# The norm of a Conformer module in another order, with its tap diagonals made inside the module

## Chip, cores, metric

One core of a Trainium2 chip. The metric is the device time of one execution in microseconds (us).

## What is computed

Two trunk layers over 256 latent tokens of 1024 channels. Layer 0 mixes tokens with a state-space scan, layer 1 with a Conformer convolution module; each is followed by a gated feed-forward network (FFN 0, FFN 1), and a norm ends it. The change lies in layer 1's module and touches the end of FFN 0:

```python
def conformer_conv_module(h, rows, w_pw1, b_pw1, dw_w, dw_b, ln_g, ln_b, w_pw2, b_pw2):
    u = h @ w_pw1 + b_pw1
    u = u[..., :CONF_DIM] * jax.nn.sigmoid(u[..., CONF_DIM:])
    v = dwconv1d(u, dw_w, dw_b) if rows is None else axial_dwconv(u, rows, dw_w, dw_b)
    v = jax.nn.silu(layernorm(v, ln_g, ln_b))
    return v @ w_pw2 + b_pw2
```

The 256 tokens form 4 grid rows of 64. `axial_dwconv` runs 31 taps along the grid row for channels 0 to 511 (horizontal) and along the 4 rows for channels 512 to 1023 (vertical). `layernorm` goes over the 1024 channels of a token.

## The kernel before

**Products.** Every large product is done as three matmuls on split operands (`mm3`): high part by high part (L293), low part of one by high part of the other (L294) and the reverse (L295). A weight tile of 128x1024 goes through four steps: SP loads it into one of four raw buffers, `wraw` (L267); ACT casts it to the high part `wh` (L269); DVE subtracts to get the low part `wl` (L282); TensorE uses both. A raw buffer is free again when its `wl` has been written, so each load waits for the subtraction four weights back. SP, ACT and DVE each work in the order of their queue.

**The module (`conformer`).** The 1024 channels are 8 blocks of 128; blocks 0 to 3 are horizontal, 4 to 7 vertical. The first projection (`w_pw1`) yields two blocks with their gates at a time; `gated` turns them around with TensorE transposes of `ug`, ACT takes the sigmoid `sig` (L1124) and DVE multiplies (L1126) into `upad` (blocks 0 to 3, with a margin) or `uver` (blocks 4 to 7). Vertical taps are done on DVE (L1107) after a first one on ACT (L1104). Of the horizontal taps, block 0's and part of block 3's are done on DVE (L1157, in the even sum `cv` and the odd sum `odd`, added on L1159; first ones on ACT, L1153 and L1155). Those of blocks 1 and 2, and the rest of block 3's, are done on TensorE (`horizontal`, L1177): `upad` is written to DRAM (L1166), read back in four shifted copies `u4` (L1168), and 32-column matmuls with diagonal matrices as weights sum the taps in PSUM. ACT (L1181, blocks 1 and 2) or DVE (L1183, block 3) moves the sum to `cv`. A call of `horizontal` takes a range of grid rows: two rows are 128 tokens, one half of the tokens.

**The diagonals.** `taps` makes three tiles of 128x1024, one each for blocks 1, 2 and 3, from the tap weights `dwx` (three DVE operations, L1086). It runs in FFN 0's second projection and puts them into buffers of the pool `ar`, which otherwise takes the weights of the modulation vectors that are worked out in the background (`araw`, loads on L368). The pool is held from FFN 0 to the end.

**The norm.** A `LayerNorm` for each half of the tokens. The table of strings `LNO` sets the order on TensorE, DVE, ACT and GpSimd, by tokens of a letter, the half (for `h` the block), and the part:

- `s`: TensorE transposes two blocks of `cv`, DVE takes their statistics (L195)
- `r`: mean and variance (L199, L451) and the root on GpSimd (L444)
- `m`: DVE normalizes 256 channels (L205)
- `c`: TensorE turns these back, ACT applies gain, bias and SiLU to give `modv` (L217)
- `x`: DVE splits `modv` into high and low part, `xmh` and `xml` (L298, L299)
- `h`: a call of `horizontal`; `t`: ACT loads its SiLU table (L1219)
- `W`, `w`: load and cast, and subtraction, of one weight of the second projection (`w_pw2`)

Ahead of it `CO` lists one call, block 1, grid rows 0 and 1; the rest of the taps are `h` tokens. Outside such a written order a scheduler places instructions by priority. `LF` lists which weights, by number, are held behind a mark (`behind`, used on the cast and on the subtraction); the hold acts on the queue of the engine that the mark is on, DVE. The second projection (`project`, with bias rows from L554) takes its first four weights half by half: all of the first half of the tokens, then the second.

## Time and profile before

| | |
|---|---|
| time, median of 3 | 886.54 us (884.85 to 888.57) |
| time of the profiled execution | 884.54 us |
| its span | 882.7 us |
| mean granted TensorE clock | 0.991 |
| busy: TensorE, DVE, ACT, GpSimd | 851.3, 663.5, 501.2, 48.6 us |
| module, end of first projection to end of second | 630 to 682 us |

The profile is of one execution. Times in its views count from the start of the span; the device time is a little longer than the span. A row of the chain of waits has start, length, and what it was. A row of a timeline has start, length, engine, line, operation, output and inputs with the shape, the number of instructions in it, and in brackets how long the engine stood ahead of it and what released it. A matmul's length includes its way through the array, so starts, not lengths, tell the rate. PE is TensorE.

### The profile page before, as it was taken

To read this page: it belongs to the slowest core of one execution; us is meant where nothing else is said; L and a number is where in the kernel's file an instruction comes from. 1 tells how busy PE (TensorE), PEld (TensorE's weight loads), DVE (VectorE), ACT (ScalarE), POOL (GpSimd) and SP (SyncE) were. 2 spreads that over 40 slices of the span, in tenths; PEclk is the share of its full clock that TensorE was granted. 3 is DMA by queue.
4 is the path that set the end of the run, shared out by engine and by line. 5 is a ranking of instruction groups with operands and counts; after the bars stand their busy time and mean duration, and the time that the engine had idled before them with its cause. 6 is when DMAs were issued, how large, how long until landed. Compare 5 with 4: busy or idle time off the path is not lost.

```text
span 882.7 us, 12690 instructions
## 1 busy us (share of the span) xinstructions
PE 851.3 (96%) x4632; PEld 649.3 (74%) x4634; DVE 663.5 (75%) x1096; ACT 501.2 (57%) x847; POOL 48.6 (6%) x77
## 2 busy tenths in 40 slices
PE   8999999999999999989999999999989999999996
PEld 4576776767777777767888777878767788888885
DVE  3378689797878989789998898777966895555434
ACT  4286988597687887374444434566354754444421
POOL 1001011101001010110000000010001000000000
PEclk9999999999999999999999999999989999999999
DMA  9757856658455455458999989828545497555521
GB/s 347 310 169 252 261 187 215 215 168 262 151 185 167 144 181 178 164 185 312 376 346 337 331 321 324 285 72 281 159 148 187 150 337 252 180 179 189 189 74 48
DMA packets 55872, 194.59 MB, mean 220 GB/s; under 512 B 6665, under 2 KB 9169, under 8 KB 54786
## 3 DMA queue, kind: packets, MB, share of 16 engines
q1 hardware_dynamic: 54338, 190.00, 63.0%
q0 software_dynamic: 896, 2.28, 0.8%
q10 hardware_dynamic: 576, 1.51, 0.5%
q8 instruction: 36, 0.59, 0.3%
q14 instruction: 26, 0.21, 0.1%
HBM read 191.94 MB, written 1.82 MB: 220 GB/s over the span
## 4 chain that ended last, share of the span: by engine, by line
PE 71%; DVE 14%; ACT 6%; DMA 5%; issue 2%; POOL 1%; SPq 0%; POOLq 0%; DVEq 0%; ACTq 0%
PE acc L295 19%; PE acc L294 19%; PE acc L293 19%; DVE wl L282 3%; DVE bx L739 3%; PE ps L251 3%; PE pa L342 2%; ACT wh L269 2%; PE ps L987 2%; PE ps L1017 1%; PE ps L1177 1%; DMA wraw<-in_w_pw_dram 1%; DMA wraw<-in_w_z_dram 1%; PE ps L1025 1%; DMA emat<-edram 1%
## 5 line engine op out<-in xcount | busy, mean ns | idle before, releaser
L282 DVE TENSOR_TENSOR wl<-wraw,wh 128x1024 fp32r<-128x1024 f32 (+2 forms) x226 | 267.4, 1189 | 94.8 <-ACT wh L269 93.8
L269 ACT CAST wh<-wraw 128x1024 fp32r<-128x1024 f32 (+2 forms) x226 | 227.7, 1016 | 154.7 <-PE acc L295 60.0
L293 PE MATMUL acc<-wh,xmh 128*128 128x512 f32 x544 | 219.0, 403 | 1.6 <-ACT bx L732 1.6
L295 PE MATMUL acc<-wh,xml 128*128 128x512 f32 x544 | 214.6, 395 | 0.9 <-DVE xml L299 0.8
L294 PE MATMUL acc<-wl,xmh 128*128 128x512 f32 x544 | 214.7, 395 | 0.5 <-DVE wl L282 0.4
L293 PEld LDWEIGHTS acc<-wh,xmh 128*128 128x128 f32 x544 | 102.5, 188 | 29.0 <-issue 4.4
L295 PEld LDWEIGHTS acc<-wh,xml 128*128 128x128 f32 x544 | 102.4, 188 | 26.5 <-DVE xml L299 3.2
L294 PEld LDWEIGHTS acc<-wl,xmh 128*128 128x128 f32 x544 | 102.7, 189 | 23.0 <-DVE wl L282 1.8
L293 PE MATMUL acc<-xmh,wh 128*128 128x512 f32 (+1 forms) x192 | 77.6, 404 | 0.1
L295 PE MATMUL acc<-xmh,wl 128*128 128x512 f32 (+1 forms) x192 | 75.4, 396 | 1.2 <-DVE wl L282 1.2
L294 PE MATMUL acc<-xml,wh 128*128 128x512 f32 (+1 forms) x192 | 75.6, 394 | 0.0
L739 DVE SCALAR_TENSOR_TENSOR bx<-bxraw,pc,bx 128x508 f32<-128x508 f32 (+1 forms) x96 | 69.8, 766 | 5.4 <-ACT bx L732 5.2
L294 PE MATMUL acc<-wl,midh 128*128 128x512 f32 x176 | 69.6, 395 | 0.6 <-DVE wl L282 0.6
L295 PE MATMUL acc<-wh,midl 128*128 128x512 f32 x176 | 69.1, 393 | 0.0
L382 DVE SCALAR_TENSOR_TENSOR araw<-araw,srow 128x1024 f32<-128x1024 f32 x56 | 67.9, 1216 | 0.0
L293 PE MATMUL acc<-wh,midh 128*128 128x512 f32 x176 | 65.9, 394 | 0.0
L293 PEld LDWEIGHTS acc<-xmh,wh 128*128 128x128 f32 (+1 forms) x192 | 35.7, 186 | 13.6 <-issue 5.1
L295 PEld LDWEIGHTS acc<-xmh,wl 128*128 128x128 f32 (+1 forms) x192 | 35.5, 186 | 10.8 <-DVE wl L282 1.9
L294 PEld LDWEIGHTS acc<-xml,wh 128*128 128x128 f32 (+1 forms) x192 | 35.8, 186 | 8.3 <-issue 1.0
L294 PEld LDWEIGHTS acc<-wl,midh 128*128 128x128 f32 x176 | 33.0, 188 | 9.8 <-DVE wl L282 2.5
L293 PEld LDWEIGHTS acc<-wh,midh 128*128 128x128 f32 x176 | 33.0, 188 | 7.4
L295 PEld LDWEIGHTS acc<-wh,midl 128*128 128x128 f32 x176 | 33.0, 188 | 7.3
(236 smaller groups left out, 1084.1 us busy)
## 6 DMA issues: line engine op xcount, KB each, us to landing
wraw<-in_ffn_in_dram SPq DMA_DIRECT2D x88, 512.0 KB, 5.0
araw<-in_ada_wt_dram SPq DMA_DIRECT2D x56, 512.0 KB, 5.2
wraw<-in_ffn_out_dram SPq DMA_DIRECT2D x44, 512.0 KB, 3.9
wraw<-in_w_xb_dram SPq DMA_DIRECT2D x32, 384.0 KB, 4.0
wraw<-in_ada_w_dram SPq DMA_DIRECT2D x24, 512.0 KB, 4.4
emat<-edram SPq DMA_DIRECT2D x8, 1536.0 KB, 7.9
wraw<-in_w_pw_dram SPq DMA_DIRECT2D x24, 512.0 KB, 4.8
araw<-in_ada_dram SPq DMA_DIRECT2D x16, 512.0 KB, 8.4
```

Source lines behind the costliest of these rows:

```text
L251: self.nc.tensor.transpose(out, in_, self.ident[0:n, 0:n])
L269: nc.scalar.copy(out=wh[:, :n], in_=raw[:, :n])
L282: self.nc.vector.tensor_tensor(out=wl, in0=raw, in1=wh.bitcast(F32), op=ALU.subtract)
L293: mm(out=out, lhsT=ah, rhs=bh, start=first, stop=False)
L294: mm(out=out, lhsT=ah, rhs=bl, start=False, stop=False)
L295: mm(out=out, lhsT=al, rhs=bh, start=False, stop=last)
L342: self.nc.tensor.matmul(out=pa[32 * j:32 * j + 32, 0:n], lhsT=self.sc[:, k, :], rhs=rhs(j), start=k == 0, stop=k == KD - 1, tile_position= ...
L382: self.nc.vector.scalar_tensor_tensor(out=raw, in0=raw, scalar=1.0, in1=self.srow, op0=ALU.mult, op1=ALU.mult, accum_out=col[:, k])
L739: nc.vector.scalar_tensor_tensor(out=o[:, :, a:b], in0=r[:, :, a + d:b + d], scalar=w(k), in1=o[:, :, a:b], op0=ALU.mult, op1=ALU.add)
L987: nc.tensor.matmul(out=ph, lhsT=bt[:, tt], rhs=xw[:, tt], start=tt == 0, stop=tt == 1)
L1017: nc.tensor.matmul(out=po[64 * j:64 * j + 64, d * 256:d * 256 + 256], lhsT=h0[:, d, c], rhs=cc, start=True, stop=True, tile_position=(0, 6 ...
L1025: nc.tensor.matmul(out=py[64 * j:64 * j + 64, p2, q * P:q * P + P], lhsT=xs[:, tt, hl * 64:hl * 64 + 64], rhs=e[:, hl, slot], start=slot i ...
```

## The change

It has five parts. First, the diagonals are made in the module, in a tile of its own (`dk`): two after the second `upad`, one after the fourth; `taps` goes, and `dwx` is loaded in the module. Second, the pool `ar` is opened anew in each FFN. Third, block 1 is done in one call with all four grid rows (256 columns), and `h11` goes. Fourth, the tokens `W` and `w` go from `LNO`: the weights of the second projection come from `project` alone, the first held behind the mark `m01`, the second behind `x00`, the other six behind `x01` (before, the last four behind `x01`, and the first four where their tokens stood). Fifth, the rest of `LNO` is put in another order: block 3's second part and the statistics of the second half come before `x01`.

```diff
-LF = (4, 8, "x01"),
+LF = (0, 1, "m01"), (1, 2, "x00"), (2, 8, "x01")
...
-CO = (1, 0, 2),
-LNO = "W0 w0 W1 w1 s02 s12 h20 h30 t00 s03 s00 s01 r00 W2 W3 s13 h11 m00 c00 m01 w2 c01 h21 x00 w3 s10 x01 m02 c02 m03 c03 x02 x03 h31 s11 r10 m10 c10 m11 c11 x10 m12 x11 m13 c12 x12 c13 x13"
+CO = (1, 0, 4),
+LNO = "s02 s12 h20 h30 t00 s03 s00 s01 r00 s13 h21 m00 c00 m01 c01 h31 x00 s10 s11 r10 x01 m02 c02 m03 c03 x02 x03 m10 c10 m11 c11 x10 m12 x11 m13 c12 x12 c13 x13"
...
-    def ffn(self, es, l, xh, xl, h, mid, then, quiet=None):
+    def ffn(self, es, l, xh, xl, h, mid, then):
         nc, t = self.nc, self.t
+        self.ar = es.enter_context(self.tc.tile_pool(name="ar", bufs=AR))
...
-            if k == kn - QUIET and quiet:
-                self.settle()
-                quiet()
-            wh, wl = ready[k] if k < len(ready) else self.weights(wsrc[k], (1, 1024), spare.get(k))
+            wh, wl = self.weights(wsrc[k], (1, 1024), spare.get(k))
...
-    def taps(self):
-
-
-        nc = self.nc
-        dwx = self.sb.tile([P, P], F32, name="dwx")
-        nc.sync.dma_start(out=dwx, in_=self.t["dwx"])
-        self.dk = []
-        for b in (1, 2, 3):
-            self.dk.append(self.ar.tile([P, 1024], F32, name="araw").rearrange("p (i c) -> p i c", i=32))
-            nc.vector.tensor_tensor(out=self.dk[-1], in0=self.diag.unsqueeze(1).broadcast_to([P, 32, 32]),
-                                    in1=dwx[:, b * 32:b * 32 + 32].unsqueeze(2).broadcast_to([P, 32, 32]), op=ALU.mult)
-
...
+        dk = cp.tile([P, 3, 32, 32], F32, name="dk")
...
+        dwx = cp.tile([P, P], F32, name="dwx")
+        nc.sync.dma_start(out=dwx, in_=t["dwx"])
...
+                i = nc.vector.scalar_tensor_tensor(out=u[:, :, 15:79] if blk < 4 else u, in0=rows(pt[:, 0:256]),
+                                                   scalar=col(PC_BPW1 + blk), in1=rows(sig), op0=ALU.add, op1=ALU.mult)
...
+            for b in ((1, 2), (3,), (), ())[j]:
+                with tc.issue_after(i.ins):
+                    nc.vector.tensor_tensor(out=dk[:, b - 1], in0=self.diag.unsqueeze(1).broadcast_to([P, 32, 32]),
+                                            in1=dwx[:, b * 32:b * 32 + 32].unsqueeze(2).broadcast_to([P, 32, 32]),
+                                            op=ALU.mult)
...
-            ready = []
             for tok in LNO.split():
-                if tok[0] == "W":
-                    ready.append(self.load(t["w_pw2"][int(tok[1])]))
-                    continue
-                elif tok[0] == "w":
-                    self.low(*ready[int(tok[1])])
-                    continue
...
-        self.count, self.fences = 4, [(a, b, ends if m is None else (marks[m],)) for a, b, m in LF]
-        self.project(es, t["w_pw2"], KD, xh, xl, (1, 2), h, then, bias=brow, by_tile=True,
-                     ready=[[x.unsqueeze(1) for x in w[1:]] for w in ready])
+        self.count, self.fences = 0, [(a, b, ends if m is None else (marks[m],)) for a, b, m in LF]
+        self.project(es, t["w_pw2"], KD, xh, xl, (1, 2), h, then, bias=brow, by_tile=True)
...
-            self.ar = pool(name="ar", bufs=AR)
             self.bg = [self.vector(0, 5, False)] + [self.vector(1, i, False) for i in range(5)]
...
-                self.ffn(es, 0, xh, xl, h, es.enter_context(tc.tile_pool(name="mid", bufs=1)), mod(1, 0, F2), self.taps)
+                self.ffn(es, 0, xh, xl, h, es.enter_context(tc.tile_pool(name="mid", bufs=1)), mod(1, 0, F2))
```

On ACT, the rows around the SiLU table's load (before: L1219) up to the modulation of the second half. `sig` is a gate, `cv<-uver` a first vertical tap, `cv<-ps` a block's taps moved out of PSUM, `wh` a weight's cast. Before:

```order
L1104 ACTIVATE cv<-uver,pc 128x256 x2
L1181 ACTIVATE cv<-ps,pc 128x128
L1219 ACT_TABLE_LOAD
L1219 ACTIVATE table<-mhalf 128x2
L269 CAST wh<-wraw 128x1024 x4
L1181 ACTIVATE cv<-ps,pc 128x128 x2
L217 ACTIVATE modv<-ps,pc 128x128 x4
L1181 ACTIVATE cv<-ps,pc 128x128
L269 CAST wh<-wraw 128x1024
L217 ACTIVATE modv<-ps,pc 128x128 x4
L269 CAST wh<-wraw 128x1024
L217 ACTIVATE modv<-ps,pc 128x128 x8
```

Now, with L1207 for the table, L1176 for the taps and L1094 for the vertical ones:

```order
L269 CAST wh<-wraw 128x1024 x2
L1176 ACTIVATE cv<-ps,pc 128x128
L1207 ACT_TABLE_LOAD
L1207 ACTIVATE table<-mhalf 128x2
L1176 ACTIVATE cv<-ps,pc 128x256
L1176 ACTIVATE cv<-ps,pc 128x128
L217 ACTIVATE modv<-ps,pc 128x128 x4
L269 CAST wh<-wraw 128x1024
L217 ACTIVATE modv<-ps,pc 128x128 x4
L269 CAST wh<-wraw 128x1024 x2
L217 ACTIVATE modv<-ps,pc 128x128 x4
L269 CAST wh<-wraw 128x1024
```

Two of the casts that stood behind the table's load stand ahead of block 2's taps (the first `cv<-ps`), two are further back, and block 1's taps (now 128x256) follow the load. Two casts in a row stand ahead of the third `modv` group, which belongs to the second half of the tokens.

On DVE, the rows from the second `upad` to the third and fourth. `upad` is a gated block, `wl` a weight's subtraction, `cv` and `odd` tap steps of block 0. Before:

```order
L1126 SCALAR_TENSOR_TENSOR upad<-ps,pc,sig 128x4x64
L282 TENSOR_TENSOR wl<-wraw,wh 128x1024 x2
L1157 SCALAR_TENSOR_TENSOR cv<-upad,pc,cv 128x256 x2
L282 TENSOR_TENSOR wl<-wraw,wh 128x1024
L1157 SCALAR_TENSOR_TENSOR odd<-upad,pc,odd 128x256
L1157 SCALAR_TENSOR_TENSOR cv<-upad,pc,cv 128x256
L282 TENSOR_TENSOR wl<-wraw,wh 128x1024
L1157 SCALAR_TENSOR_TENSOR odd<-upad,pc,odd 128x256
L1157 SCALAR_TENSOR_TENSOR cv<-upad,pc,cv 128x256
L1157 SCALAR_TENSOR_TENSOR odd<-upad,pc,odd 128x256
L1157 SCALAR_TENSOR_TENSOR cv<-upad,pc,cv 128x256
L282 TENSOR_TENSOR wl<-wraw,wh 128x1024
```

Now, with L1116 for `upad` and L1152 for the tap steps:

```order
L1116 SCALAR_TENSOR_TENSOR upad<-ps,pc,sig 128x4x64
L1122 TENSOR_TENSOR dk<-konst,dwx 128x1024 x2
L282 TENSOR_TENSOR wl<-wraw,wh 128x1024 x3
L1152 SCALAR_TENSOR_TENSOR cv<-upad,pc,cv 128x256
L1152 SCALAR_TENSOR_TENSOR odd<-upad,pc,odd 128x256
L1152 SCALAR_TENSOR_TENSOR cv<-upad,pc,cv 128x256
L1152 SCALAR_TENSOR_TENSOR odd<-upad,pc,odd 128x256
L1152 SCALAR_TENSOR_TENSOR cv<-upad,pc,cv 128x256
L1152 SCALAR_TENSOR_TENSOR odd<-upad,pc,odd 128x256
L1152 SCALAR_TENSOR_TENSOR cv<-upad,pc,cv 128x256
L1116 SCALAR_TENSOR_TENSOR upad<-ps,pc,sig 128x4x64 x2
L1122 TENSOR_TENSOR dk<-konst,dwx 128x1024
```

The `upad` x2 that follows the last row of before is on the last row but one of now. The two diagonals come ahead of three subtractions, those of the first projection; the two that belonged to the second are gone from here, and a third diagonal follows `upad`.

On TensorE, the taps up to the transposes for the statistics (`acc<-konst,cv`); `u_5961` and `u_5960` are copies of block 1's rows, `u_5969` and `u_5968` of block 2's, `u_5989` and `u_5988` of block 3's, and `nrm` is a normalized row turned back. Before:

```order
L1177 MATMUL ps<-u_5961,araw 32x128
L251 MATMUL acc<-konst,cv 128x128 x3
L251 MATMUL ps<-konst,ug 128x128 x6
L1177 MATMUL ps<-u_5961,araw 32x128 x16
L1177 MATMUL ps<-u_5969,araw 32x128 x32
L1177 MATMUL ps<-u_5961,araw 32x128 x15
L1177 MATMUL ps<-u_5989,araw 32x128 x20
L251 MATMUL acc<-konst,cv 128x128 x8
L1177 MATMUL ps<-u_5961,araw 32x128 x32
L251 MATMUL ps<-konst,nrm 128x128 x4
L1177 MATMUL ps<-u_5969,araw 32x128 x32
```

Now:

```order
L1172 MATMUL ps<-u_5960,dk 32x256
L251 MATMUL ps<-konst,ug 128x128 x6
L1172 MATMUL ps<-u_5960,dk 32x256 x8
L1172 MATMUL ps<-u_5968,dk 32x128 x32
L1172 MATMUL ps<-u_5960,dk 32x256 x23
L1172 MATMUL ps<-u_5988,dk 32x128 x20
L251 MATMUL acc<-konst,cv 128x128 x8
L1172 MATMUL ps<-u_5968,dk 32x128 x32
L251 MATMUL ps<-konst,nrm 128x128 x4
L1172 MATMUL ps<-u_5988,dk 32x128 x20
L251 MATMUL acc<-konst,cv 128x128 x2
```

Block 1 has one set of 32 matmuls of 256 columns in place of two of 128, and the second set, which stood behind the transposes, is gone; block 3's last 20 have come forward to the first `nrm`.

More of the change, by code (lines that the diff above doesn't have):

```diff
@@ L503, in ffn, with project @@
         self.rate = R_OUT
-        self.project(es, t["ffn_out"][l], KF, mh, ml, (l, 5), h, then, between=lambda: turn(*last.pop()), quiet=quiet)
-    def project(self, es, wsrc, kn, ah, al, gate, h, then=None, rs=None, bias=None, early=None, by_tile=False, between=None,
-                quiet=None, ready=()):
+        self.project(es, t["ffn_out"][l], KF, mh, ml, (l, 5), h, then, between=lambda: turn(*last.pop()))
+    def project(self, es, wsrc, kn, ah, al, gate, h, then=None, rs=None, bias=None, early=None, by_tile=False, between=None):
         nc = self.nc
@@ L1176, in horizontal @@
                 for g in range(4):
-                    nc.tensor.matmul(out=x[32 * g:32 * g + 32], lhsT=self.dk[blk - 1][:, g * 8 + i],
+                    nc.tensor.matmul(out=x[32 * g:32 * g + 32], lhsT=dk[:, blk - 1, g * 8 + i],
                                      rhs=rows(u4[:, g])[:, r0:r0 + nr, 4 * i:4 * i + 64], start=i == 0, stop=i == n - 1,
```

2 lines of the change are left out of this document (removed).

## Prediction

> **What bounds the kernel now.** I read the page first: the span, and which engine carries the chain that ended last.
>
> ```profile
> span 882.7 us, 12690 instructions
> ...
> PE 71%; DVE 14%; ACT 6%; DMA 5%; issue 2%; POOL 1%; SPq 0%; POOLq 0%; DVEq 0%; ACTq 0%
> ```
>
> TensorE carries 71% of that chain, so only time in which TensorE stands, or works at half clock, can be won. The table of the times says that this execution took 884.54 us, of which 882.7 are span; 1.84 lie around it. All sums below are made on its clock. The median of the three runs shown, 886.54, lies 2.00 above, and I add that at the end.
>
> Next, the chain of waits around the module's norm, which the change rewrites. Columns: start, length, what.
>
> ```profile
> 639.90 1.28 ACT L1219
> ...
> 641.40 3.78 ACT wh L269 x4
> ...
> 647.60 3.52 PE ps L1177 x64
> ...
> 651.71 1.88 PE ps L1177 x64
> ```
>
> ACT loads a table and casts four raw weights in one piece, 3.78 us, before it may move block 1's taps out of PSUM. All that TensorE does meanwhile is wait. Its own timeline has both gaps, in brackets, and its rate outside them.
>
> ```profile
> 632.89 0.30 PE L251 MATMUL acc<-konst,cv 128*128 128x128 f32 x1 [2.06 <-DVE cv L1107]
> ...
> 636.02 5.38 PE L1177 MATMUL ps<-u,araw 128*32 128x128 f32 x166
> ...
> 645.49 0.47 PE L251 MATMUL acc<-konst,cv 128*128 128x128 f32 x1 [3.61 <-ACT cv L1181]
> ...
> 653.89 0.49 PE L554 MATMUL acc<-bh,onerow 1*128 1x512 f32 x1
> ...
> 654.55 0.50 PE L293 MATMUL acc<-wh,xmh 128*128 128x512 f32 x1
> ...
> 667.13 0.62 PE L293 MATMUL acc<-wh,xmh 128*128 128x512 f32 x2
> ...
> 674.67 0.39 PE L293 MATMUL acc<-wh,xmh 128*128 128x512 f32 x1
> ...
> 681.63 0.39 PE L293 MATMUL acc<-wh,xmh 128*128 128x512 f32 x1
> ...
> 682.32 0.82 PE L251 MATMUL ps<-konst,nrm 128*128 128x128 f32 x6
> ```
>
> From 674.67 to 681.63 stand 30 full matmuls: 0.232 us each. The first of the last projection starts at 654.55, its last ends where the six transposes of 682.32 begin. TensorE stands 2.06 us before block 4's columns are there and 3.61 before block 1's. The granted clock (the column behind POOL's) shows what follows each gap:
>
> ```profile
> 634.00:636.00 2.00, 2.00 (x9) 1.69 (x9) 1.58 (x4) 0.50 (x2) 0.00 (x0) 0.50 0.00 0
> 636.00:638.00 2.00, 2.00 (x53) 1.89 (x56) 1.72 (x5) 1.61 (x4) 0.00 (x0) 0.68 0.00 0
> ...
> 648.00:650.00 2.00, 2.00 (x44) 1.85 (x40) 1.67 (x5) 0.00 (x0) 0.55 (x1) 0.50 0.03 8
> ```
>
> It is 0.50 at 634, 0.68 at 636 and 0.50 again at 648. That is why 64 tap records of one size take 3.52 us at 647.60 and 1.88 at 651.71: 1.64 us lost by the second gap beside the gap itself.
>
> **The change part by part.**
>
> *Diagonals.* They leave FFN 0's second projection and come back in the module.
>
> ```profile
> L1086 DVE TENSOR_TENSOR araw<-konst,dwx x3: 1215/1220/1220, 538.4 to 545.3; 128x1024 f32<-128x1024 f32 x3
> ```
>
> ```profile
> 535.00:548.00 13.00, 12.62 (x54) 9.70 (x53) 12.82 (x16) 6.55 (x7) 0.00 (x0) 1.00 0.87 301
> ```
>
> The old three, 1.22 each, stood under a TensorE that was busy 12.62 of 13 us; removing them brings 0, and would bring at most the 0.38 that it stood there. In the module they take time of a DVE on the path. Its timeline has the start after the second `upad` and the third; the chain has what one large operation and one tap step take of its time when others follow on:
>
> ```profile
> 607.09 1.23 DVE L282 TENSOR_TENSOR wl<-wraw,wh 128x1024 fp32r<-128x1024 f32 x1
> ...
> 617.25 0.87 DVE L1126 SCALAR_TENSOR_TENSOR upad<-ps,pc,sig 128x256 f32<-128x256 f32 x2
> ```
>
> ```profile
> 613.48 1.14 DVE wl L282
> ...
> 624.45 0.40 DVE odd L1157
> ```
>
> The new order is two diagonals, three subtractions, seven tap steps, and then the gated rows (`upad` x2): 607.09 + 5 x 1.14 + 7 x 0.40 = 615.6. Before, the same `upad` began at 617.25: five subtractions stood ahead of it too (two of them W0's and W1's of the last projection), one tap step more, and the rest was idle time. So DVE could be 1.6 earlier. But ACT may not be ready. Its queue holds the casts of W0 and W1 ahead of the gates that `upad` needs:
>
> ```profile
> 612.13 1.05 ACT L269 CAST wh<-wraw 128x1024 fp32r<-128x1024 f32 x1 [0.29 <-DMA wraw<-in_w_pw_dram]
> 613.93 1.05 ACT L269 CAST wh<-wraw 128x1024 fp32r<-128x1024 f32 x1 [0.75 <-DMA wraw<-in_w_pw_dram]
> 614.89 0.83 ACT L1124 ACTIVATE sig<-ps,pc 128x256 f32<-128x256 f32 x2
> ...
> 639.53 0.37 ACT L1181 ACTIVATE cv<-ps,pc 128x128 f32<-128x128 f32 x1 [1.71 <-PE ps L1177]
> ```
>
> ```profile
> 608.34 4.70 SPq L267 DMA_DIRECT2D wraw<-in_w_pw_dram  x3
> ...
> 651.59 3.06 SPq L267 DMA_DIRECT2D wraw<-in_w_pw_dram  x2
> ```
>
> ```profile
> DMA to landing us min/median/max: 3.5/4.9/7.0
> ```
>
> ```profile
> 656.20 1.05 ACT L269 CAST wh<-wraw 128x1024 fp32r<-128x1024 f32 x1 [2.17 <-DMA wraw<-in_w_pw_dram]
> ```
>
> W1's raw slot is released by the subtraction that stood at 607.09. Two diagonals now stand ahead of it (2.28), so its load is issued at 610.55 where it was 608.34. What it takes is not known: 3.5 to 7.0 us in this stretch, median 4.9; for W1 itself 608.34 to 613.93, 5.6, with W0's under way beside it; for the load of 651.59, with no other weight in flight, 656.20 - 651.59 = 4.6. W0's will be nearly through, so I take 4.6. Then cast 0.95 (the spacing of casts that follow on: 613.93 to 614.89) and first gate 0.47 end at 616.6, and DVE stands 1.0 us; at 3.5 it would not stand, at 7.0 it would stand 3.5.
>
> From `upad` to block 4's columns (TensorE starts on them at 632.89) it took 15.6 us. It now has the third diagonal (+1.14) and three tap steps fewer ahead of that (24 for 27, -1.19). So 616.6 + 15.55 = 632.15 against 632.89: **0.7 us gained** ahead of the norm, no more.
>
> *The norm's first part.* Two matmuls of the first projection that used to be done before the gap now come behind it (2 x 0.232), so the tap records begin 0.25 earlier, near 635.8. Block 1 comes as 32 taps of 256 columns where it was 32 of 128. What the wider form costs is bounded by two rows of other work:
>
> ```profile
> 253.56 0.64 PE L342 MATMUL pa<-wraw,sc 128*32 128x256 f32 x8
> ...
> 11.98 0.64 PE L342 MATMUL pa<-araw,sc 128*32 128x128 f32 x16
> ```
>
> Eight records of 256 columns take as long as sixteen of 128: 0.64. So block 1 costs two halves, 2 x 1.88 warm, and the half that used to follow the norm (3.52, cold) is paid here: +1.9. If only issue counted, it would be nothing; I take 1.9, as the row says. The records of 636.02, 5.38 us, become 7.2, and TensorE has all three blocks at 643.0. Block 2's come off first as before, ACT's table load follows, and now nothing stands between it and block 1's eviction: the casts of two weights stand ahead of block 2's, where ACT stood 1.71 (its row of 639.53, above). So the 3.61-us stall goes, and what is late next is TensorE itself. Statistics, mean and normalization:
>
> ```profile
> 641.81 0.43 DVE L195 BATCH_NORM_STATS2 bnst<-acc 128x6 f32<-128x256 f32 x1
> 646.00 0.43 DVE L195 BATCH_NORM_STATS2 bnst<-acc 128x6 f32<-128x256 f32 x1 [3.76 <-PE acc L251]
> ...
> 648.80 0.99 DVE L205 TENSOR_SCALAR nrm<-acc,bnmv,rstd 128x256 f32<-128x256 f32 x2 [0.33 <-POOL rstd L444]
> ```
>
> From the first of these on (641.81) there was a wait of 3.76; without it the path to the normalized row is 648.80 - 641.81 - 3.76 = 3.2 us. It starts at 643.4 and gives 646.6 against 648.80: **2.2 gained**. Of the 3.6 stall, 1.9 went into the wider taps, and 0.2 to 0.5 came from above.
>
> *Behind it.* Block 2's second half follows without a gap, so warm: 1.88 for 3.52. Block 1's second half is gone from here. Then transposes, block 3's last 40, two bias rows; the first matmul of the projection comes near 650.4 where it was 654.55: **4 us ahead**.
>
> *Given back.* W0 and W1 are subtracted here now, on a DVE that also has the statistics of the other half of the tokens pulled forward. In the new order, from 646.6 to the end of the fourth subtraction: three pairs' worth of normalized rows and splits (0.91 + 0.67 + 0.67 + 0.91), four subtractions (4.56), one eviction and its wait (0.7), statistics (1.3), one cast (0.3): 10.0 us, 656.6. (A pair of normalized rows is 648.80's 0.99 less the overlap with the next; a split is the 0.67 from 666.67 to 667.34, below; statistics are three of 641.81's 0.43; the eviction with its wait is an estimate from TensorE's 40 records of block 3, 40 / 64 x 1.88 = 1.2, of which DVE's subtraction covers the larger part.) That subtraction frees the slot of the weight whose cast stands in ACT ahead of the second half's first modulation. Load 4.6, cast 1.05, modulation to matmul as in before:
>
> ```profile
> 665.83 1.51 ACT L217 ACTIVATE modv<-ps,pc 128x128 f32<-128x128 f32 x4 [6.25 <-PE ps L251]
> ```
>
> ```profile
> 666.67 0.29 DVE L298 CAST xmh<-modv 128x256 fp32r<-128x256 f32 x1 [1.03 <-ACT modv L217]
> ...
> 667.34 0.54 DVE L205 TENSOR_SCALAR nrm<-acc,bnmv,rstd 128x256 f32<-128x256 f32 x1
> ```
>
> From 665.83 to 667.13 it takes 1.3, of which 0.1 overlaps the cast. So the second half starts at 656.6 + 4.6 + 1.05 + 1.2 = 663.4. Until then TensorE does the 25 matmuls that need only the first half and then stands. What is left is 67 x 0.232 + 0.66 bias (653.89 to 654.55) + 0.7 transposes = 16.9. The end is 680.3 against 682.32: **2.0 us gained**. This is the step that I trust least: each us of a load counts here once, and once more at W1.
>
> *The rest.* FFN 0's own tiles for background loads move to another place in memory and open with it; its first loads go out ahead of one weight whose slot is not free yet. The load of `dwx` is now in a queue whose next weight waits for its slot anyway. Background loads no longer stand ahead of the last two weights in SP. I count these 0, within 0.4 either way. At the end of the stage DVE has one more subtraction between two row updates; the projection's last matmuls, which run until 682.32 in the old trace, cover it; without that cover it would cost its 1.14.
>
> **The sum:** 884.54 - 2.0 = 882.5 profiled, 884.5 on the median.
>
> **The rivals.**
> (a) *Loads are quick.* At 3.5 us both waits shrink by 1.1: 2.2 more, 882.3. For it: in both places fewer weights are in flight than at 608.34. Against: the two loads whose issue and landing are quoted took 4.6 and 5.6.
> (b) *TensorE is quicker ahead of the norm.* If the wide taps cost only their issue, the norm comes 1.9 earlier, against the two rows of 0.64. Or TensorE stays warm: the first gap, 2.06 us, was followed by clock 0.50 at 634 and 0.68 at 636, which cost 1.0 + 0.6 = 1.6. If the shorter gap lets the clock stand, the norm comes 1.6 earlier. Either gives about 882.8. The Trainium skill ("TensorE: Matmul & The Clock Gate", Part 1: The HAM clock gate) says that the clock halves after an idle window of about 3.4 us, which runs freely. By that rule the clock should have stood at 634 already; the trace disagrees, with 0.50 after 2.06, and I follow the trace, in which only the 3.61-us case fits.
> (c) *The ring of raw weights and ACT's order decide, and it is slower.* At 7.0, the longest load here, DVE stands 2.4 more at W1 and the second half starts 2 x 2.4 later: 680.3 + 4.8 = 685.1, 2.8 over before, 889.3. It decides from 2.0 / 2 = 1.0 more than 4.6, a load of 5.6, which W1's own was. For it: casts in ACT's queue that wait for a load hold everything behind; 656.20 shows one. Against: W1's 5.6 shared its time with W0's.
> (d) *Cold again.* If the transposes between the taps and block 2's second half, with their waits for statistics, are idle enough for 0.50, its 1.64 are not won and block 3's 40 records cost 1.1 more: 2.7 less, 887.2. Against: no wait there is over 1 us without ACT's casts.
> (e) *It does not do what it says:* the stretch is bound by DVE in another way and the time does not move: 886.5.
>
> **How the numbers follow.** A measurement of this kernel can tell about 0.5% (4.4 us) from no change. Chances: forecast 0.42 (its own range 883.3 to 885.7, from 0.4 elsewhere and 0.3 us in the two loads), (a) 0.18, (b) 0.12, (c) 0.14, (d) 0.08, (e) 0.06. The faster side of 882.1 is reached by half of (a) and (b), 0.15, and by a tenth from the forecast and unknown gains elsewhere: 0.26. Slower by as much, over 891.0, needs (c) with more behind it: 0.07. The rest, 0.67, is no change by that measure. The range reaches from (a) with part of (b), 881.0, to most of (c), 888.5.
>
> **What would show it.** Right: no four casts in a row behind the table load; block 1's eviction next to it; a normalized row near 646.6; 0.50 only once; `upad` x2 with a wait of about 1 on the gate; a cast waiting for a load ahead of the second half, and TensorE idle before 663. Wrong: if the 256-column records run at the pace of the 128-column ones, the norm is 1.9 earlier; if the second half starts by 661 or after 666, the load was misjudged.

## The result, and the profile after

The changed kernel takes 880.17 us (median of 8; 879.33 to 883.09), the kernel before in the same runs 885.27: ratio 0.9941, 95% interval 0.9918 to 0.9964. Two later sets of the same kernel gave 0.9937 (0.9916 to 0.9958) and 0.9960 (0.9940 to 0.9981). All three intervals hold 0.9940 to 0.9958, which is faster by 3.7 to 5.3 us of 885.27; the forecast was 884.5 for a kernel before of 886.54, a gain of 2.0, and its range began at 881.0. Of the about 4.4 us by which the time lies under the forecast, 1.3 come from the kernel before, whose median is 885.27 here; the other 3.1 are gain that was not foreseen (5.1 for 2.0). A gain of 5.1 would itself have stood in the range, which reached to 5.5. One of the ten executions of the kernel before in the run before_again, 2936 us long, counts as slow and is left out of its ratio.

The span fell from 882.7 to 877.3 us. The shares of the chain that ended last tell nothing of the change: TensorE's was 71% and 61% in two profiles of the kernel before, and 61%, 64% and 74% in three of the changed one (the repeated profiles are before_again, after_again and after_third, below).

TensorE's timeline in the changed kernel, with the row of normalized columns at the module's start, and that of the kernel before beside it:

```profile
586.68 0.66 PE L251 MATMUL ps<-konst,nrm 128*128 128x128 f32 x4 [0.81 <-ACT wh L269]
...
632.11 0.30 PE L251 MATMUL acc<-konst,cv 128*128 128x128 f32 x1 [1.30 <-DVE cv L1097]
...
634.99 6.53 PE L1172 MATMUL ps<-u,dk 128*32 128x256 f32 x166
...
643.32 1.96 PE L1172 MATMUL ps<-u,dk 128*32 128x128 f32 x64
645.49 0.86 PE L251 MATMUL ps<-konst,nrm 128*128 128x128 f32 x4 [0.21 <-DVE nrm L205]
...
659.76 0.50 PE L293 MATMUL acc<-wh,xmh 128*128 128x512 f32 x1 [0.20 <-DVE xmh L298]
...
676.75 0.97 PE L251 MATMUL ps<-konst,nrm 128*128 128x128 f32 x6
```

```profile
586.20 0.66 PE L251 MATMUL ps<-konst,nrm 128*128 128x128 f32 x4 [0.83 <-ACT wh L269]
```

The gap of 3.61 us is gone and none over 1.30 is left. From 586.20 to 682.32 the module took 96.1 us; from 586.68 to 676.75 it takes 90.1, so 6.0 were won inside it; what lies around it is 0.6 us longer in this profile. Taps, 166 records, take 6.53. The granted clock:

```profile
634.00:636.00 2.00, 2.00 (x28) 1.18 (x30) 1.73 (x5) 0.98 (x3) 0.00 (x0) 1.00 0.00 0
636.00:638.00 2.00, 2.00 (x76) 1.91 (x73) 2.00 (x8) 2.00 (x4) 0.00 (x0) 1.00 0.03 8
...
650.00:652.00 2.00, 1.22 (x3) 0.48 (x3) 1.90 (x8) 1.05 (x1) 1.01 (x2) 1.00 0.42 98
652.00:654.00 2.00, 1.79 (x8) 1.04 (x9) 2.00 (x5) 1.33 (x4) 0.12 (x1) 1.00 0.75 299
```

It is 1.00 where the kernel before had 0.50 (half clock; a stretch at half clock is called cold below) and 0.68, although a gap of 1.30 us stands ahead of it. ACT, around the table load and at the two loads on which the forecast rested:

```profile
615.15 1.05 ACT L269 CAST wh<-wraw 128x1024 fp32r<-128x1024 f32 x1 [1.96 <-DMA wraw<-in_w_pw_dram]
...
636.86 1.98 ACT L269 CAST wh<-wraw 128x1024 fp32r<-128x1024 f32 x2
638.74 0.35 ACT L1176 ACTIVATE cv<-ps,pc 128x128 f32<-128x128 f32 x1
639.10 1.28 ACT L1207 ACT_TABLE_LOAD   x1
...
640.51 0.46 ACT L1176 ACTIVATE cv<-ps,pc 128x256 f32<-128x256 f32 x1
...
657.62 1.05 ACT L269 CAST wh<-wraw 128x1024 fp32r<-128x1024 f32 x1 [2.51 <-DMA wraw<-in_w_pw_dram]
658.57 1.50 ACT L217 ACTIVATE modv<-ps,pc 128x128 f32<-128x128 f32 x4
```

Block 1's eviction (640.51) follows the table, as foreseen, and the casts stand where the order said. The rows of DVE, and the load that the cast of 657.62 waits for:

```profile
616.61 0.88 DVE L1116 SCALAR_TENSOR_TENSOR upad<-ps,pc,sig 128x256 f32<-128x256 f32 x2 [0.54 <-ACT sig L1114]
...
644.79 1.00 DVE L205 TENSOR_SCALAR nrm<-acc,bnmv,rstd 128x256 f32<-128x256 f32 x2 [0.33 <-POOL rstd L444]
645.71 1.22 DVE L282 TENSOR_TENSOR wl<-wraw,wh 128x1024 fp32r<-128x1024 f32 x1
...
648.86 1.21 DVE L282 TENSOR_TENSOR wl<-wraw,wh 128x1024 fp32r<-128x1024 f32 x1
...
652.39 1.22 DVE L282 TENSOR_TENSOR wl<-wraw,wh 128x1024 fp32r<-128x1024 f32 x1
...
653.73 1.22 DVE L282 TENSOR_TENSOR wl<-wraw,wh 128x1024 fp32r<-128x1024 f32 x1
```

```profile
653.68 0.33 SPq L267 DMA_DIRECT2D wraw<-in_w_pw_dram  x1
```

The last row is SP's, from its timeline: the load was issued at 653.68, behind the third subtraction of the second projection's weights (652.39 and 1.22), and landed 3.94 us later, when the cast began (657.62).

### The profile page after: what moved, and what is told of

The parts are those of the page before. It is cut to its first block, busy times and chain, and to the rows that moved or that the text cites. A ratio compares the mean times of both kernels' runs of the same rounds, so it can differ in the third digit from the quotient of the medians.

```text
span 877.3 us, 12573 instructions
## 1 busy us (share of the span) xinstructions
PE 847.5 (97%) x4570; PEld 643.4 (73%) x4570; DVE 662.3 (75%) x1096; ACT 501.5 (57%) x846; POOL 49.1 (6%) x77
## 3 DMA queue, kind: packets, MB, share of 16 engines
q0 software_dynamic: 896, 2.28, 0.8%
## 4 chain that ended last, share of the span: by engine, by line
PE 61%; DVE 17%; ACT 6%; DMA 6%; issue 3%; POOL 1%; POOLq 0%; SPq 0%; DVEq 0%; ACTq 0%
PE acc L295 17%; PE acc L294 17%; PE acc L293 17%; DVE wl L282 4%; DVE bx L736 3%; PE ps L251 2%; ACT wh L269 2%; DMA wraw<-in_w_z_dram 2%; DMA wraw<-in_ffn_out_dram 2%; PE ps L1014 1%; PE ps L984 1%; DMA wraw<-in_w_pw_dram 1%; PE ps L1022 1%; PE pa L342 1%; PE ps L1172 1%
```

## The experiments

In the runs below "module" is the time from the third row of normalized columns at its start (586.20 and 586.68 above) to the six transposes at its end (682.32 and 676.75), and "norm" the time from the same start to the first transposes of normalized channels on TensorE (651.05 and 645.49). In before, before_again, weights_back, order_only, diag_only and halves TensorE did 64 or 128 tap records between DVE's columns and these transposes, so "norm" is late there by TensorE's own work: on DVE the columns (L205) began 62.60 us behind the start in before, 58.11 in after, 57.07 in halves. Both times come from one profiled execution each; the ratio comes from all executions against the kernel before. "Gap" is TensorE's first wait, for block 4's columns, "clock" what was granted behind it, 1.00 or down to 0.50. Runs that end in _again, _2 and _third are repeated profiles of one kernel.

| run | gap | clock | norm | module | ratio (95%) |
|---|---|---|---|---|---|
| before | 2.06 | 0.50 | 64.85 | 96.12 | |
| before_again | 1.85 | 0.50 | 64.69 | 96.03 | 0.9993 (0.9978 to 1.0007) |
| after | 1.30 | 1.00 | 58.81 | 90.07 | 0.9941 (0.9918 to 0.9964) |
| after_again | 0.59 | 1.00 | 58.14 | 90.77 | 0.9937 (0.9916 to 0.9958) |
| after_third | 1.25 | 1.00 | 58.77 | 91.38 | 0.9960 (0.9940 to 0.9981) |
| weights_back | 1.97 | 0.50 | 64.68 | 94.94 | 0.9983 (0.9964 to 1.0001) |
| order_only | 2.49 | 0.50 | 64.99 | 95.27 | 0.9973 (0.9958 to 0.9988) |
| weights_only | 1.58 | 1.00 | 57.62 | 94.08 | 1.0015 (0.9995 to 1.0035) |
| weights_only_2 | 1.66 | 1.00 | 57.68 | 95.79 | 1.0028 (1.0002 to 1.0054) |
| casts_later | 1.59 | 1.00 | 57.39 | 93.30 | 0.9997 (0.9968 to 1.0025) |
| weights_grow | 1.24 | 1.00 | 57.28 | 91.10 | 0.9938 (0.9919 to 0.9958) |
| diag_only | 1.13 | 1.00 | 60.95 | 91.85 | 0.9971 (0.9950 to 0.9991) |
| diag_back | 1.03 | 1.00 | 58.52 | 89.85 | 0.9974 (0.9952 to 0.9995) |
| halves | 1.40 | 1.00 | 59.23 | 90.78 | 0.9944 (0.9923 to 0.9964) |
| taps_first | 0.74 | 1.00 | 58.51 | 91.14 | 0.9948 (0.9927 to 0.9969) |
| w0_early | 2.12 | 0.50 | 61.13 | 92.69 | 0.9939 (0.9918 to 0.9960) |
| dk_behind | 2.40 | 1.00 | 59.92 | 91.16 | 0.9939 (0.9918 to 0.9960) |

The theory was that TensorE's stall behind ACT's four casts, with the cold stretch that follows, is what the change takes away. The rivals were that the order of the norm itself, the diagonals, or the loads make the difference.

**Do the weights stand in the way? weights_back, weights_only, casts_later.** The first is the changed kernel with the tokens of the weights back in `LNO` and the old holds (both cut here):

```diff
-LF = (0, 1, "m01"), (1, 2, "x00"), (2, 8, "x01")
+LF = (4, 8, "x01"),
-LNO = "s02 s12 h20 h30 t00 s03 s00 s01 r00 s13 h21 ...
+LNO = "W0 w0 W1 w1 s02 s12 h20 h30 t00 s03 s00 s01 r00 W2 W3 s13 h21 ...
```

> The changed kernel with the fourth part undone: four weights loaded, cast and subtracted at written places in the norm's order again. Theory 1: the four casts stand behind the table's load again, a gap of about 3 us opens ahead of block 1's columns with clock 0.50 after it; 4 to 6 us slower than the changed kernel, near before or up to 2 us over it, since the diagonals now come on top on DVE. Theory 2 (the order itself carries half of the gain): only 2 to 3 us slower than the changed kernel.

Its ratio is 0.9983, 3.7 us slower than the changed kernel, and its norm as late as before. TensorE's timeline:

```profile
633.88 0.30 PE L251 MATMUL acc<-konst,cv 128*128 128x128 f32 x1 [1.97 <-DVE cv L1098]
...
648.07 0.37 PE L251 MATMUL acc<-konst,cv 128*128 128x128 f32 x1 [3.04 <-ACT cv L1177]
```

The gap behind ACT's eviction is back with 3.04 us, and so is the first theory's main step. The other four parts of the change together leave a module 1.2 us shorter than before, no more than three profiles of the changed kernel differ among themselves (90.07 to 91.38).

The second is the kernel before with its weights taken out of `LNO` and held as in the changed kernel:

```diff
-LF = (4, 8, "x01"),
+LF = (0, 1, "m01"), (1, 2, "x00"), (2, 8, "x01")
-LNO = "W0 w0 W1 w1 s02 s12 ...
+LNO = "s02 s12 ...
```

> The kernel before with only the fourth part of the change: no weights of the second projection in the norm's order, all of them held behind the marks on DVE. Theory 1 (the gain is TensorE's stall behind the four casts and the cold stretch after it): no four casts between the table's load and block 1's eviction, the 3.61-us gap gone, clock 1.00 there; DVE also has two subtractions fewer ahead of block 4, so the first gap of 2.06 shrinks too. 4 to 7 us faster than before, near 880. Theory 2 (the gain is the other order of the norm, and block 1 in one call): 0 to 2 us faster. Theory 3 (the loads decide): the casts that wait for loads now stand ahead of modulations and eat it, 0 to 3 us faster.

The norm came 7.2 us earlier than before, more than in the changed kernel, and yet the kernel is not faster: 1.0015, and 1.0028 when it was taken again. Of the 7.2 us 2.0 and 0.3 were left at the module's end. DVE, TensorE and GpSimd show where much of the rest went:

```profile
674.02 0.69 DVE L573 TENSOR_TENSOR res<-acc,grow 128x512 f32<-128x512 f32 x1 [3.31 <-DMA grow<-gdram]
```

```profile
674.77 0.49 PE L554 MATMUL acc<-bh,onerow 1*128 1x512 f32 x1 [3.00 <-DVE res L573]
```

```profile
666.29 0.55 POOL L444 TENSOR_TENSOR rstd<-var,mhalf 128x1 f32<-128x1 f32 x1 [16.63 <-DVE var L451]
666.79 0.64 POOL L430 DMA_DIRECT2D grow<-gdram  x1
```

A row update (`res`, L573) stands in DVE's queue ahead of the last normalized columns of the second half. It waits 3.31 us for the gate row `grow`, a row of factors by which the update multiplies, which GpSimd loads behind the root of the second half (666.29, issued at 666.79). In the old order that root is late, and everything behind the row update waits with it. In the changed kernel the same load was issued at 651.49, since the second half's statistics stand earlier; its GpSimd timeline:

```profile
650.99 0.55 POOL L444 TENSOR_TENSOR rstd<-var,mhalf 128x1 f32<-128x1 f32 x1 [6.23 <-DVE var L451]
651.49 0.64 POOL L430 DMA_DIRECT2D grow<-gdram  x1
```

The second profile of weights_only shows what such a wait can cost besides: it was 2.88 us on TensorE, and the clock fell behind it, where it had stayed at 1.00 behind the 3.00 us of the first; its module is 1.7 us longer. First profile, then second:

```profile
675.00:676.00 1.00, 1.00 (x6) 0.56 (x6) 0.96 (x4) 0.00 (x0) 0.00 (x0) 1.00 0.00 0
```

```profile
671.00:672.00 1.00, 0.56 (x1) 0.50 (x2) 1.00 (x3) 0.00 (x0) 0.00 (x0) 0.65 0.00 0
672.00:673.00 1.00, 1.00 (x3) 0.41 (x2) 0.96 (x3) 0.00 (x0) 0.00 (x0) 0.50 0.00 0
```

In the third, only the loads and casts of the third and fourth weight move behind the first normalized columns of the kernel before:

```diff
-... s01 r00 W2 W3 s13 h11 m00 c00 m01 w2 c01 ...
+... s01 r00 s13 h11 m00 c00 m01 W2 w2 c01 W3 ...
```

> The kernel before with one thing moved: the loads and casts of the third and fourth weight of the second projection, which stood at written places ahead of the first half's normalized columns, come behind them; the first two weights stay early, the diagonals, the other steps and block 1's two calls stay. Theory 1 (ACT's four casts in a row are the stall): the gap of 3.61 us and the cold stretch behind it go, the first normalized row comes 4 to 6 us earlier in the module; but the late root of the second half, its gate row's load and a row update written ahead of the last normalized columns remain, so only 1 to 3 us are left at the module's end. Theory 2 (the stall is TensorE's or DVE's own work behind the table): no earlier.

The norm came 7.5 us earlier, the module ended 2.8 earlier, with 2.63 us of the same wait and a cold stretch behind it; the ratio is 0.9997. Both runs say that the stall at the casts is real and that taking it away alone is worth nothing that can be measured.

**Is it the gate row? weights_grow.** The kernel of weights_only with one statement more, which ties the gate row's load to the first half's root:

```diff
-        self.count, self.fences = 0, [(a, b, ends if m is None else (marks[m],)) for a, b, m in LF]
+        self.pmark = marks["r00"]; self.count, self.fences = 0, [(a, b, ends if m is None else (marks[m],)) for a, b, m in LF]
```

> The run with only the weights held back (which won 7.2 us up to the first normalized row of the module and ended only 2.0 ahead), with one thing more: the load of the gate row on GpSimd's queue is tied to the first half's root and no longer to the second half's. Theory 1 (part of what was given back is the wait of 3.3 us on DVE, 3.0 on TensorE, for that load, which the old order issues only after the second half's root): that wait goes, 2 to 3 us faster than the run with only the weights. Theory 2 (the late second half is what costs): the wait turns into one of the same length elsewhere, 0 to 0.7 us faster.

The module went from 94.08 and 95.79 to 91.10, the ratio from 1.0015 to 0.9938. With its weights held back and its gate row loaded early, the old order is as fast as the changed kernel, without a wait over 0.44 us behind the norm. In this run, then, the new order is not needed for its own sake, and neither are the diagonals' new place and block 1's one call: the order is one way to have the second half's root, and the load behind it, in time. The two kernels' times differ by 6.8 to 8.0 us, more than the 3.0 to 4.7 of the module; the profiles do not show the rest.

**The order alone: order_only.** The kernel before with block 1 in one call and the changed order, the weights' tokens kept in it:

> The kernel before with only block 1 in one call and the new order of the norm's other steps; weights at their written places, diagonals in FFN 0. Theory 1 (the stall behind the four casts must go before anything else): the gap of about 3 us and the cold stretch stay; the second half's statistics come earlier but nobody needs them earlier; 0 to 1.5 us faster than before in the module. Theory 2 (the order is the gain): 3 to 5 us faster.

The stall was there with 2.00 us, after it the cold stretch (64 records in 3.62), the norm no earlier. 0.85 us in the module; its ratio, 0.9973, is more than that.

**The diagonals: diag_only, diag_back, dk_behind.** In the first only the diagonals and the pool `ar` move, as in the change; in the second they are undone in the changed kernel; in the third the two first ones come later:

```diff
-            for b in ((1, 2), (3,), (), ())[j]:
+            for b in ((), (1, 2, 3), (), ())[j]:
```

> The kernel before with only the diagonals moved into the module and the background pool opened in each FFN. Theory 1: three operations of 1.14 us more on DVE ahead of block 4's columns, of which the load wait of W1 hides part; the first gap grows from 2.06 to 3 to 4 us, 1 to 3 us slower than before, 886 to 888. Rival (the freed queue and memory help elsewhere, so that this part carries gain): 0.5 to 2 us faster than before.

> The changed kernel with its diagonals made in FFN 0 again and the background pool held as before. Theory 1: 3.4 us less on DVE ahead of block 4, the first gap of 1.30 goes, and as TensorE is nearly without gaps behind the norm, 0.8 to 1.5 us faster than the changed kernel, near 879. Rival: a background load stands ahead of the last two weights again and the second half of the projection waits for it: same or up to 2 us slower than the changed kernel.

The first was expected slower and is faster, 4.3 us in the module, 0.9971 by the runs. Its first gap was 1.13 and the clock stayed at 1.00 behind it. And the scheduler put block 1's eviction elsewhere, as ACT's timeline shows:

```profile
637.62 0.37 ACT L1177 ACTIVATE cv<-ps,pc 128x128 f32<-128x128 f32 x1
639.36 0.37 ACT L1177 ACTIVATE cv<-ps,pc 128x128 f32<-128x128 f32 x1 [1.38 <-PE ps L1173]
639.75 1.28 ACT L1215 ACT_TABLE_LOAD   x1
...
641.15 3.87 ACT L269 CAST wh<-wraw 128x1024 fp32r<-128x1024 f32 x4
```

Both evictions stand ahead of the table's load here, so the casts do not hold up block 1's. TensorE still stood once, and the clock fell to 0.50 behind it, but for DVE:

```profile
644.88 0.63 PE L251 MATMUL acc<-konst,cv 128*128 128x128 f32 x4 [2.99 <-DVE bnst L195]
```

DVE was busy with tap steps until 643.66 and took the statistics from 643.98 on. Whether that is the diagonals' price is not shown. This was not one part alone: with DVE's work moved, the order on ACT changed with it, and what it says of the diagonals' own price is little. The second run says more: without them in the module its length is 89.85, against 90.1 to 91.4 with them. Three operations of 1.14 us cost 0.2 to 1.5 there, by one profile against three. Its ratio, 0.9974, is nevertheless worse than the changed kernel's; its profile does not show why.

> The changed kernel with the two diagonals that stood ahead of the first projection's last three subtractions put behind the third and fourth gated block, beside the third diagonal; TensorE's order is the same. Theory 1 (the two diagonals hold up the subtraction that frees the second weight's raw slot, its load holds up ACT's gates, and these hold up DVE ahead of block 4: the wait on the gate was 0.54 and 0.24 us in the two profiles of the changed kernel, with a first gap of 1.30 and 0.59; in the run with the early first subtraction it was 1.11, the gap 2.12 and the clock fell to 0.50): the wait on the gate goes, the first gap is under 1 us, the clock stays at 1.00, and the module from its first normalized columns to the end of the second projection takes 89.5 to 90.5 us; 0.3 to 1 us faster than the changed kernel. Theory 2 (the gap has another cause, as DVE's sum of work is the same): the gap stays at 1.0 to 2.1 us; same as the changed kernel.

The wait on the gate went, as the first theory said, and the gap was not shorter for it: 2.40 us, where the changed kernel had 0.59 to 1.30; the ratio, 0.9939, is the changed kernel's. DVE's timeline:

```profile
611.08 1.23 DVE L282 TENSOR_TENSOR wl<-wraw,wh 128x1024 fp32r<-128x1024 f32 x1 [1.13 <-ACT wh L269]
...
613.49 1.22 DVE L282 TENSOR_TENSOR wl<-wraw,wh 128x1024 fp32r<-128x1024 f32 x1 [0.27 <-ACT wh L269]
...
618.59 0.87 DVE L1116 SCALAR_TENSOR_TENSOR upad<-ps,pc,sig 128x256 f32<-128x256 f32 x2
619.38 3.48 DVE L1122 TENSOR_TENSOR dk<-konst,dwx 128x1024 f32<-128x1024 f32 x3
```

It now stands 1.13 and 0.27 us ahead of subtractions, for the casts, where the changed kernel has its diagonals. This theory of the gap falls; what sets the gap stays open. At their place the two diagonals, 2.28 us, fill time of which DVE would wait 1.40 anyway.

**Block 1's call: halves.** `CO = (1, 0, 2),` and `h11` back ahead of `h21` in the changed kernel.

> The changed kernel with block 1 in two calls again (two grid rows ahead of the norm, two behind the first statistics). Theory 1 (256 columns cost two times 128, so the one call puts 1.9 us ahead of the norm): the first normalized row 1.2 to 1.9 us earlier, given back by the second call of 1.9 behind it; 0 to 0.5 us to either side of the changed kernel at the module's end. Theory 2 (the one call saves time of TensorE): 1 to 2 us slower.

Module 90.78, ratio 0.9944: the same as the changed kernel. One call of 256 columns costs what two of 128 do. On DVE the first normalized columns came earlier, as theory 1 says, though a little less than it says:

```profile
642.99 1.00 DVE L205 TENSOR_SCALAR nrm<-acc,bnmv,rstd 128x256 f32<-128x256 f32 x2 [0.33 <-POOL rstd L444]
```

That is 11.52 us behind block 4's columns (631.47), for 12.68 in the changed kernel. TensorE turned them back no earlier, since the second call of block 1 stood in between.

**Can more be had? taps_first, w0_early.** In the first `h20` stands ahead of `s02 s12`; in the second the marks are changed:

```diff
-LF = (0, 1, "m01"), (1, 2, "x00"), (2, 8, "x01")
+LF = (0, 1, None), (1, 2, "m01"), (2, 8, "x01")
```

> The changed kernel with block 2's first taps written ahead of the first statistics (the token h20 first), so that TensorE does not stand in its order behind transposes whose columns DVE has not finished. Theory 1 (what is left of the gap ahead of the norm is lost time of TensorE): the 1.30-us gap goes, 0.8 to 1.3 us faster than the changed kernel. Theory 2 (DVE's vertical taps of blocks 6 and 7 set the norm anyway): same within 0.4 us. Theory 3: one cast now stands between the table's load and block 1's eviction, 0.95 us, and eats the gain: 0 to 1 us slower.

> The changed kernel with the first weight's subtraction held only behind the last taps on DVE, where DVE stood 1.1 us, and the second weight's behind the first half's normalized columns. Theory 1 (behind the norm DVE is the bound: it is busy 1.9 of 2 us from 648 to 662 while TensorE is busy 1.2 of 2 between 650 and 652): TensorE's holes at 650 to 652 close, the third load is issued 1 us earlier, no cold stretch at 652 as in the second profile of the changed kernel; 0.7 to 1.5 us faster than the changed kernel. Theory 2: the cast of the fifth weight now stands in ACT ahead of block 2's second eviction and waits for its load; same or up to 1 us slower.

Neither beats the changed kernel by what can be measured: 0.9948 and 0.9939 against 0.9941. In taps_first the gap of 0.74 waited for gated rows, and the clock fell to 0.50 later, behind the norm. In the profiled execution of w0_early, the longest of its twelve (888.06 us; median 880.52), the gap was 2.12 us and the taps ran cold:

```profile
640.00:642.00 2.00, 2.00 (x10) 1.00 (x10) 2.00 (x6) 0.58 (x1) 0.00 (x0) 0.66 0.00 0
642.00:644.00 2.00, 2.00 (x14) 1.24 (x16) 0.77 (x3) 1.13 (x3) 0.00 (x0) 0.50 0.00 0
```

```profile
639.18 0.30 PE L251 MATMUL acc<-konst,cv 128*128 128x128 f32 x1 [2.12 <-DVE cv L1097]
...
643.18 6.90 PE L1172 MATMUL ps<-u,dk 128*32 128x256 f32 x166
```

```profile
653.36 1.00 DVE L205 TENSOR_SCALAR nrm<-acc,bnmv,rstd 128x256 f32<-128x256 f32 x2 [0.33 <-POOL rstd L444]
```

This prices the clock, since TensorE's order up to the norm is the changed kernel's. From block 4's columns to the first normalized ones it took 14.18 us (639.18 to 653.36). The three profiles of the changed kernel took 12.68, 12.69 and 12.68, and dk_behind, with the longer gap of 2.40 but the clock at 1.00, took 12.69. So the cold stretch costs 1.5 us there, and the length of the gap ahead of it does not count in it.

**Does the clock belong to the kernel? after_again, before_again, after_third, weights_only_2.** All four are unchanged copies.

> The changed kernel, unchanged, beside the others on this chip. 4 to 6 us faster than before, as measured; in its profile the module from its first normalized columns to the end of the second projection is 6 us shorter than in the kernel before (90.1 for 96.1), and the state-space layer, whose order is the same in all these kernels, starts the module within 3 us of the other profiles.

> The kernel before, profiled a second time. If the half-clock stretches belong to the kernel: a first gap of 2.0 to 2.2 us, 0.50 behind it and again behind the gap of 3.6; the module from its first normalized columns to the end of the second projection 96.1 us within 0.5. If they belong to the execution: the second stretch (gap 3.6) comes again, the first may be missing and the module then is 1.5 us shorter. The part ahead of the module within 1 us of 586.2 if its length belongs to the kernel, up to some us off if not.

> The changed kernel, profiled a third time. If the half-clock stretch of its second profile (0.50 from 653 to 656) belongs to the execution: 1.00 throughout or one such stretch, the module 90.0 to 90.8 us. If the gap ahead of the norm alone decides: 1.00 behind it whenever it is under 2 us.

> The run with only the weights held back, profiled a second time. If the length ahead of the module belongs to the kernel: 592 to 593 us again, where the kernel before has 586. If it belongs to the execution: 585 to 590. The module near 94.1 us again, with the wait of 3 us for the gate row's load, since that has a cause in the order.

The kernel before fell again behind each of its two gaps, 1.85 and 3.61 us, and its module was the same within 0.1. The changed kernel fell once in its second and third profile, between 652 and 657, and not in its first; these two modules are 0.7 and 1.3 us longer. The second profile:

```profile
650.00:652.00 2.00, 1.18 (x5) 0.39 (x3) 1.93 (x7) 0.82 (x1) 1.14 (x2) 1.00 0.72 229
652.00:654.00 2.00, 1.97 (x6) 1.33 (x7) 2.00 (x3) 1.92 (x5) 0.00 (x0) 0.77 0.83 246
654.00:656.00 2.00, 2.00 (x6) 1.56 (x5) 2.00 (x5) 0.51 (x1) 0.00 (x0) 0.50 0.92 262
```

TensorE was busy 1.18 of 2 us from 650 to 652 there, and 1.22 in the first profile, where the clock stayed. And dk_behind kept 1.00 behind the longest first gap of all but one:

```profile
634.38 0.30 PE L251 MATMUL acc<-konst,cv 128*128 128x128 f32 x1 [2.40 <-DVE cv L1097]
```

```profile
634.00:636.00 2.00, 1.62 (x10) 1.18 (x11) 2.00 (x8) 0.58 (x1) 0.00 (x0) 1.00 0.00 0
636.00:638.00 2.00, 2.00 (x24) 1.09 (x24) 1.73 (x5) 0.84 (x3) 0.00 (x0) 1.00 0.00 0
```

So a stretch at half clock belongs partly to the execution. The length ahead of the module, which was expected to tell whether it is the kernel's or the execution's, was 586.67 in before_again and 589.77 in weights_only_2 (592.77 in its first profile): it differs by 3 us between executions of one kernel, and by another 3 between the two kernels, whose order ahead of the module is the same. By the expectations the first speaks for the kernel and the second for the execution, so this stays open.

## Why the prediction was wrong

Its direction and its places were right; its size was not, and one mechanism was not in it. Point by point:

- *The casts.* Right: the stall goes, block 1's eviction follows the table, and weights_back brings it back (3.04 us).
- *DVE ahead of the norm.* Nearly right. The gate's wait was forecast at 1.0 and was 0.54 (load 4.09 us from 611.06 to 615.15, where 4.6 was taken). That 632.15 was forecast for block 4's columns and 632.11 measured is partly luck: the module began 0.48 us later in this profile, and the wait was 0.46 shorter. Counted from the module's start, block 4's columns came 1.26 us earlier than before, for 0.7 foreseen.
- *The first normalized columns.* This is the step that failed most: forecast 646.6, measured 644.79. It let the clock fall behind the first gap as before and kept that cold stretch in the transposes and the taps ("The records of 636.02, 5.38 us, become 7.2"), 14.45 us from block 4's columns (632.15) to 646.6. At a clock of 1.00 this took 12.68; in w0_early, cold, 14.18. The taps took 6.53, and the transposes ahead of them were quicker for the same reason: the taps began 2.88 us behind block 4's columns (632.11 to 634.99), where they had begun 3.13 behind (632.89 to 636.02), with two matmuls more in between. The price of 256 columns was right: 6.53 less 104 records at 1.88 / 64 us leaves 3.5 us for block 1's 62, against 1.8 for 62 of 128 columns, and halves agrees. Its rival (b), with a chance of 0.12, named this case and priced it well, at 1.6.
- *The fourth subtraction.* Also wrong: the sum to its end was right, 10.0 for 10.16, but the slot of the weight that ACT waits for, the seventh, came free with the third, so the load was issued at 653.68; from the first normalized columns to the end of the third subtraction it is 8.8 us, not 10.0.
- *The load.* Mis-sized: 3.94 for the 4.6 taken, so that rival (a) came in part. The second half began at 659.76 for 663.4, which is the prediction's own sign of a misjudged load ("by 661"), and from there to the end it was 16.99 us for 16.9. By the three terms: 1.8 from the norm, 1.2 from the subtraction, 0.7 from the load make 3.7 of the 3.64 that it came earlier. TensorE, which was to stand until then, waited 0.20 us: matmuls of the first half filled the time.
- *What was not seen.* The gate row's load behind the second half's root (weights_only, weights_grow). The prediction took the new order's early root as work pulled forward on DVE, and priced it only so. In weights_only, where it stays in its old place, it cost 3 us of waiting, and no gain was left.
- *The rivals on the other side.* (c), loads of 7 us, did not come: 4.09 and 3.94. (d), a cold stretch among the later taps, did not come there either, but two of three profiles had one a little later (652 to 657).

The prediction set the Trainium skill ("TensorE: Matmul & The Clock Gate", Part 1: The HAM clock gate) aside, since 0.50 followed a gap of 2.06 where the page asks for an idle window of about 3.4 us. That was too quick. The page also says that the window is free-running, so that the same work can meet it differently, and with this the runs agree: one kernel fell in two of three profiles, 2.40 and 3.00 us passed without a fall, 1.85 did not. That it needs a whole window without work they do not bear out: the changed kernel fell with no gap over 0.51 us, in a stretch where TensorE was busy six tenths of the time (1.18 of 2 us). Nearer to that is what the Trainium skill's same page says under "A second HAM failure mode: psum-queue depth-cycling", that many short idles between groups of matmuls can bring the clock down too; there it is told of another kind of kernel. weights_grow, which fell at 666 out of stretches in which TensorE was busy 1.83 and 2.00 of 2 us, speaks for neither.

What stays open: the medians and the modules agree for most runs to about 2 us, but not for diag_back, casts_later and weights_only, whose modules are 6.3, 2.8, and 2.0 and 0.3 us shorter than before, and whose medians are 2.3 us shorter for the first and not measurably shorter for the others. All three keep the pool `ar` as before; so does weights_grow, whose median shows its gain. The record also has the mean granted clock of every execution. In every set the longer executions tend to have the lower clock (correlation -0.42 to -0.94). By set it averages 0.992 to 0.994 in weights_only and casts_later and 0.994 in before_again, 0.995 to 0.997 in the changed kernel's three sets and 0.997 in weights_grow; a cold stretch of 3.4 us takes 0.002 off it. So the executions of weights_only and casts_later seem to hold one or two such stretches more than the changed kernel's, which would fit the wait for the gate row, behind which the clock fell in two of three profiles. That is argued, not shown, and for diag_back (0.996) it explains nothing.

## What to carry to other kernels

A stall that ends in an in-order queue is worth what the next one in line leaves of it: holding the casts back won 7 us at the norm and nothing at the end until the load that hung on a later root was freed too. So follow each engine's queue to the end of the stage, GpSimd's with its one DMA included, and ask of every moved step which loads are tied to it. And where TensorE idles for about two us or more, take a cold stretch as a chance and work out both times: ahead of the norm it was worth 1.5 us here.

## What the runs showed of the hardware

- Behind a first gap of 0.59 to 1.66 us (11 profiles) the granted clock stayed at 1.00; behind 1.85, 1.97, 2.06, 2.12 and 2.49 it fell to 0.50; behind 2.40 it did not. Of the later gaps, it fell behind 2.00, 2.63, 2.88, 2.99, 3.04 and 3.61 (twice), and not behind 3.00 (weights_only). So the length of the gap alone does not decide.
- Each stretch at half clock in the modules lasted 3.4 us, or twice that: 3.40 to 3.42 in thirteen cases, and 6.82 to 6.84 in three (before, before_again, weights_only_2), summed from the mean clock of stretches of 1 us.
- It also fell without a gap over 0.51 us, in two of three executions of the changed kernel, where TensorE was busy 1.18 and 1.45 of 2 us just before (and 1.22 in the one that did not fall), and in weights_grow at 666, where it had been busy 1.83 and 2.00 of 2 us. So the share of busy time alone does not decide either.
- A 32-column-tile fp32 record of 256 columns takes 0.055 us, one of 128 columns 0.029 (1.88 us for 64): the columns count, not the number of records.
- In kernels that differ only behind that point (taps_first, w0_early) the length ahead of the module was 584.6 and 592.9 us in the profiles, the two ends of what all seventeen show.
